# The opening of an mLSTM and window-attention encoder: modulated tiles made in pairs on two engines, products taken as tiles come, the prompt's sums on GpSimd

## The chip, the cores and the metric

The kernel runs on one core of a Trainium2 chip. The metric is the device time of one execution in microseconds (us); lower is better. The engines are TensorE (PE in the profile; its weight loads are PEld), VectorE (DVE), ScalarE (ACT), GpSimd (POOL) and SyncE (SP), which here issues the DMAs.

## What is computed

A two-layer encoder runs over two sequences, a prompt of 256 tokens and a sample of 512, with 1024 channels. Each has a conditioning vector `c`; layer 0 mixes with a chunked mLSTM in both directions, layer 1 with windowed attention, and each layer ends with a convolutional feed-forward block. The part that the change touches is the start of layer 0:

```python
mod = jax.nn.silu(c) @ adaln_w[l] + adaln_b[l]
sh1, sc1, g1, sh2, sc2, g2 = [t[:, None, :] for t in jnp.split(mod, 6, axis=-1)]
h = rmsnorm(x, norm_g[l, 0]) * (1 + sc1) + sh1
...
proj = h @ w_in          # q, k, v, o and the gates of the mLSTM
```

The gates go through a log-sigmoid, a running sum and a running maximum along the tokens before the mLSTM's chunks can be weighted.

## The kernel before

**Layout.** Activations lie with channels on the 128 partitions and tokens along the free axis: eight channel tiles (`KC = 8`) of 768 tokens, the prompt in columns 0 to 255, the sample in 256 to 767. `RANGES` cuts the tokens into three ranges of 256: two of the sample, then the prompt.

**Products.** Each operand is split into a high part (`hh`, `whi`; rounded to the fast float format) and a low part (`hl`, `wlo`; the rest). A product of two tiles is three matmuls: high weight with high activation, high with low, low with high. `fp_copy_split` (L255) makes the parts: a cast on ACT, a subtraction on DVE. In the profile `hh` and `hl` are named `zh` and `zl`.

**Order.** Most instructions are ordered by a planner that simulates a time line at build time and lets whatever is ready there go first, by place in the program; each engine then runs its own queue strictly in that order. Inside a `manual_schedule` block the named engines take the order in which the code is written, and `issue_after` puts an instruction behind another on its engine.

**The opening, in `first` (L1508).** The sample's ranges are loaded and normalized (`Norm`, L89: squares on ACT, sums of tiles on POOL, the sum over partitions by small matmuls with a constant, the root on POOL, a broadcast by matmuls, a multiplication on DVE). Between them `adaln(0, 0)` (L388) multiplies the silu of `c` with sixteen weight rows of 512 KB; its result is copied out by DVE and ACT, transposed, and gives `mod` (shift) and `gain`. Then `modulate` (L561) applies gain and shift to each tile of the sample on DVE in place and splits it.

**The window, in `mlstm` (L633).** Three weight tiles go first: the gates' (`gw`) and the two halves of head 0's queries, through `window` (L310). It goes range by range, in a range weight tile by weight tile, and there over the channels; so each weight tile is finished with a range at a different time. The prompt is normalized beside it (`Norm` with all eight squares summed on TensorE, applied by `modulated`, L540): its steps are traced at points that `tick` chooses between the products. After a sequence's last range the results leave PSUM, by `gates` (L644) or by `keep` (L649). Weights are staged in `raw` tiles (five slots), their parts in `whi` and `wlo` (three slots each); small temporaries of the norms lie in `nt` tiles (eight slots).

**Behind it.** The gates run through Abs, Exp and Ln on ACT (L666 to L668) and six groups of scans and differences on DVE (L669 to L680); then come the two halves of head 0's keys (`gemmT`, L292), with four PSUM banks, and its values (`gemmN`, L331). The modulation of layer 1 (`adaln_v`, L484) fills DVE's gaps: per weight row two operations of 1024 columns, taken a row at a time.

Of the kernel before, what the change touches and what calls it, by code (L numbers as in the profile page):

```python
# [88 lines left out]
class Norm:  # L89
# [13 lines left out]
    def x(self, c):  # L103
        return self.xt[c // 4][:, c % 4, self.rng[0] : self.rng[1]]
# [62 lines left out]
class Net:  # L167
# [219 lines left out]

    def adaln(self, l, th):  # L388
# [16 lines left out]
        ps = self.ps()  # L405
        for i in range(2 * KC):
            k, h = divmod(i, 2)
            cur = fetch(i)
            for g in range(2):
                r0 = 32 * (2 * h + g)  # L410
                self.mm(
                    ps[r0 : r0 + 32, :], self.silc[:, k, :], cur[:, g * 512 : (g + 1) * 512], k == 0, k == KC - 1
                )
# [4 lines left out]
        nc.vector.tensor_copy(sb[0], ps[:, :256])  # L418
        nc.scalar.copy(sb[1], ps[:, 256:])
        pt = self.ps()  # L420
        for b in range(4):
            nc.tensor.transpose(
                pt[:, b * P : (b + 1) * P], sb[b // 2][:, (b % 2) * P : (b % 2 + 1) * P], self.ident
            )
# [5 lines left out]
        if th == 0:  # L430
            for s in range(2):
# [52 lines left out]
    def adaln_v(self, l, pool):  # L484
# [9 lines left out]
        for grp, k in rows:  # L494
# [5 lines left out]
            for s in range(2):  # L500
                w = self.silc[:, k, s : s + 1]
                if k == 0:
                    nc.vector.tensor_scalar(acc[:, s], row, w, None, ALU.mult)
                else:
                    stt(acc[:, s], row, w, acc[:, s], ALU.mult, ALU.add)  # L505
# [127 lines left out]
    def mlstm(self, pool, gw, xt):  # L633
# [211 lines left out]


# [661 lines left out]
    def first(self, pool):  # L1508
# [13 lines left out]
        for rng in RANGES[:2]:  # L1522
            self.modulate(xt, rng, 0, 0)
# [140 lines left out]
```

## The time and the profile before

| | |
|---|---|
| median of three runs | 1846.66 us (1844.48 to 1851.62) |
| profiled execution | 1845.79 us, of which the profiled span is 1843.8 |
| mean granted TensorE clock | 0.992 of full speed |
| TensorE busy | 1794.3 us, 97% |
| VectorE / ScalarE / GpSimd busy | 74% / 49% / 26% |
| DMA | 184.48 MB, 332 GB/s in the first fortieth of the span |

Times in the profile count from the start of the span. A line of the timeline gives start, length, engine, the line of the code, the operation, the tile written and those read, and in brackets how long the engine had idled and what released it. A line such as L253 is a helper's: all products made through `mm` carry it, so they are told apart by their tiles.

### The profile page before, as it was taken

To read this page: it belongs to the slowest core of one execution; us is meant where nothing else is said; L and a number is where in the kernel's file an instruction comes from. 1 tells how busy PE (TensorE), PEld (TensorE's weight loads), DVE (VectorE), ACT (ScalarE), POOL (GpSimd) and SP (SyncE) were. 2 spreads that over 40 slices of the span, in tenths; PEclk is the share of its full clock that TensorE was granted. 3 is DMA by queue.
4 is the path that set the end of the run, shared out by engine and by line. 5 is a ranking of instruction groups with operands and counts; after the bars stand their busy time and mean duration, and the time that the engine had idled before them with its cause. 6 is when DMAs were issued, how large, how long until landed. Compare 5 with 4: busy or idle time off the path is not lost.

```text
span 1843.8 us, 28933 instructions
## 1 busy us (share of the span) xinstructions
PE 1794.3 (97%) x11290; PEld 1657.0 (90%) x11290; DVE 1373.0 (74%) x2101; ACT 898.0 (49%) x1815; POOL 481.6 (26%) x386
## 2 busy tenths in 40 slices
PE   6999999999999999999999999999999999999997
PEld 3987887888998999999999999889989999999997
DVE  4755676886689777777777757766898777787776
ACT  4443443444456444444444556765564444444443
POOL 1001001021024333333331313430134333333322
PEclk8999999999999999999999999999999999999999
DMA  8343556546212221222223321124122222222212
GB/s 332 114 149 133 172 195 226 169 137 211 98 46 77 72 65 64 69 68 68 69 69 93 104 83 50 53 94 136 48 81 69 69 69 69 69 69 69 69 35 69
DMA packets 64245, 184.48 MB, mean 100 GB/s; under 512 B 6167, under 2 KB 23831, under 8 KB 64108
## 3 DMA queue, kind: packets, MB, share of 16 engines
q1 hardware_dynamic: 64108, 182.63, 30.2%
q8 instruction: 89, 1.46, 0.3%
q14 instruction: 48, 0.39, 0.1%
HBM read 176.17 MB, written 6.43 MB: 99 GB/s over the span
## 4 chain that ended last, share of the span: by engine, by line
PE 86%; DVE 6%; DMA 3%; ACT 2%; issue 1%; POOL 1%; SPq 0%; POOLq 0%; ACTq 0%
PE ps L253 27%; PE pa L253 25%; PE ps L1161 10%; PE ps L1164 10%; PE ps L1162 10%; PE pa L1000 1%; DVE wlo L260 1%; DMA raw<-in_w_dram 1%; DMA slab<-in_x_dram 1%; DVE slab L589 1%; DMA slab<-in_adaln_w_dram 1%; DVE ada L505 0%; PE pa L1162 0%; PE pa L1164 0%; PE pa L1161 0%
## 5 line engine op out<-in xcount | busy, mean ns | idle before, releaser
L259 ACT CAST whi<-raw 128x1024 fp32r<-128x1024 f32 x237 | 248.7, 1051 | 347.3 <-PE pa L253 161.4
L260 DVE TENSOR_TENSOR wlo<-raw,whi 128x1024 fp32r<-128x1024 f32 x237 | 320.5, 1353 | 114.7 <-ACT whi L259 112.5
L253 PE MATMUL pa<-slab,whi 128*128 128x256 f32 (+1 forms) x1472 | 346.5, 331 | 3.2 <-DVE slab L589 3.2
L253 PEld LDWEIGHTS pa<-slab,whi 128*128 128x128 f32 x1472 | 252.7, 188 | 27.6 <-DVE slab L589 4.7
L589 DVE SCALAR_TENSOR_TENSOR slab<-pa,mod,slab 128x256 f32<-128x256 f32 (+1 forms) x368 | 211.5, 593 | 70.8 <-PE pa L253 70.5
L253 PE MATMUL pa<-slab,wlo 128*128 128x256 f32 (+1 forms) x736 | 233.8, 330 | 0.0
L253 PE MATMUL ps<-zh,whi 128*128 128x256 f32 (+1 forms) x560 | 188.9, 338 | 1.8 <-ACT whi L259 1.2
L253 PE MATMUL ps<-zh,wlo 128*128 128x256 f32 (+1 forms) x560 | 184.0, 330 | 1.4 <-DVE wlo L260 1.4
L253 PE MATMUL ps<-zl,whi 128*128 128x256 f32 (+1 forms) x560 | 184.9, 332 | 0.0
L1161 PE MATMUL ps<-zh,whi 128*128 128x384 f32 x504 | 172.3, 342 | 3.7 <-ACT nt L1232 1.9
L1162 PE MATMUL ps<-zl,whi 128*128 128x384 f32 x504 | 169.9, 337 | 1.8 <-DVE zl L1118 1.8
L1164 PE MATMUL ps<-zh,wlo 128*128 128x384 f32 x504 | 169.0, 335 | 0.0
L253 PEld LDWEIGHTS pa<-slab,wlo 128*128 128x128 f32 x736 | 138.5, 188 | 13.1 <-DVE wlo L260 0.4
L1197 POOL TENSOR_TENSOR raw<-raw,raw 128x512 f32<-128x512 f32 x40 | 51.9, 1298 | 330.8 <-DVE wlo L260 259.4
L253 PE MATMUL ps<-slab,whi 128*128 128x384 f32 x512 | 132.3, 339 | 2.2 <-ACT sg L841 1.3
L1394 POOL TENSOR_TENSOR slab<-slab 128x772 f32<-128x772 f32 x44 | 86.4, 1967 | 171.7 <-DVE slab L1382 159.8
L1381 DVE SCALAR_TENSOR_TENSOR slab<-slab,cstt,slab 128x771 f32<-128x771 f32 x88 | 105.4, 1199 | 26.7 <-ACT slab L1379 26.6
L505 DVE SCALAR_TENSOR_TENSOR ada<-raw,silc,ada 128x1024 f32<-128x1024 f32 x84 | 112.1, 1372 | 14.5 <-DMA raw<-in_adaln_w_dram 14.4
L253 PEld LDWEIGHTS ps<-zh,whi 128*128 128x128 f32 x560 | 107.2, 192 | 15.1 <-issue 4.4
L253 PEld LDWEIGHTS ps<-zl,whi 128*128 128x128 f32 x560 | 107.3, 192 | 12.0 <-issue 3.4
L253 PEld LDWEIGHTS ps<-zh,wlo 128*128 128x128 f32 x560 | 107.2, 192 | 11.6 <-DVE wlo L260 2.3
L1194 POOL TENSOR_TENSOR raw<-raw 128x512 f32<-128x512 f32 x40 | 63.1, 1578 | 196.5 <-DMA raw<-in_w_dram 168.8
(291 smaller groups left out, 4269.5 us busy)
## 6 DMA issues: line engine op xcount, KB each, us to landing
raw<-in_w_dram SPq DMA_DIRECT2D x208, 512.0 KB, 3.7
raw<-in_adaln_w_dram SPq DMA_DIRECT2D x84, 512.0 KB, 4.5
slab<-in_x_dram SPq DMA_DIRECT2D x12, 512.0 KB, 6.5
slab<-in_adaln_w_dram SPq DMA_DIRECT2D x12, 512.0 KB, 10.3
slab<-mrows SPq DMA_DIRECT2D x8, 384.0 KB, 5.4
xs<-slab SPq DMA_DIRECT2D x6, 512.0 KB, 3.6
bt<-brow SPq DMA_DIRECT2D x16, 192.0 KB, 3.2
slab<-xs SPq DMA_DIRECT2D x6, 512.0 KB, 6.0
```

The lines of the kernel that those rows point to most:

```text
L253: self.nc.tensor.matmul(out, lhsT, rhs, start=start, stop=stop)
L259: nc.scalar.copy(hi, src)
L260: return nc.vector.tensor_tensor(lo, src, hi.bitcast(F32), ALU.subtract)
L505: stt(acc[:, s], row, w, acc[:, s], ALU.mult, ALU.add)
L589: self.nc.vector.scalar_tensor_tensor(x, o, self.mod[l][:, gc + c, q : q + 1], x, ALU.mult, ALU.add)
L1161: mm(o, wh[:, k], hi[k], start=start and k == 0, stop=False, skip_group_check=True)
L1162: mm(o, wh[:, k], lo[k], start=False, stop=False, skip_group_check=True)
L1164: mm(o, wl[:, k], hi[k], start=False, stop=k == 3, skip_group_check=True)
L1194: tt(q[2], q[2], q[3], ALU.add)
L1197: tt(q[0], q[2], q[0], ALU.subtract)
L1381: stt(y[:, 1:], u[:, :-1], w(0), y[:, 1:], ALU.mult, ALU.add)
L1394: nc.gpsimd.tensor_tensor(y, y, yrow[:, j], ALU.mult)
```

## The change

- **adaLN.** The two halves of its result are copied into two separate temporaries instead of two halves of one `raw` tile. After every channel from the fourth on, products of a constant tile with itself (`warm`) follow on TensorE into a bank that is overwritten later: six each, one after the last channel, and five more behind the last transpose. Each sequence's gain is made right behind its own shift.
- **Sample.** `modulate` is gone. In the new function `opening`, ACT modulates the odd channels (in place, by a scale and a bias) and DVE the even ones; ACT casts each tile, DVE makes the low part. All of it stands pair by pair in an order written out for TensorE, ACT and DVE. In the first range the gates' products follow each pair, those of the second weight tile one pair later, and the rest at the end; the parts of the second and third weight tile are made at fixed places in between. In the second range all three tiles' products follow each pair.
- **Prompt.** Its squares stand in the second range, four behind each of the first two pairs, and POOL adds all eight up. The sum over partitions follows the second range's products; then, channel by channel, DVE and ACT make the high part, TensorE takes six products, and low part and three products follow one channel later. All results leave PSUM at the end.
- **Layer 1.** The first rows of `adaln_v` stand behind the prompt's last low part on DVE.

```diff
+    def warm(self, o, n):
+        for _ in range(n):
+            self.mm(o[:, :P], self.ones, self.ones, True, True)
...
+            if h and k > 2:
+                with self.tc.issue_after(last.ins):
+                    self.warm(pt, 6 if k < KC - 1 else 1)
...
-        sb = self.stg.tile([P, 2, 256], F32, tag="raw", name=self.nm("sb"), bufs=5)
-        sb = [sb[:, z] for z in range(2)]
+        sb = [self.tmp([P, 256]) for _ in range(2)]
...
                 if k == 0:
-                    nc.vector.tensor_scalar(acc[:, s], row, w, None, ALU.mult)
+                    with self.tc.issue_after(self.opened.ins):
+                        nc.vector.tensor_scalar(acc[:, s], row, w, None, ALU.mult)
...
-        ws = [(gw, gates)] + [(w, keep(qt0, 0, c)) for c, w in self.halves(U_MIN)]
+        raws = [self.load(U_MIN, h) for h in range(2)]
         self.load_x(io["x"], RANGES[2:], xt)
         nc.sync.dma_start(self.kct[:, P:], io["kc"][:, P : 3 * P])
-        norm = Norm(self, xt, PROMPT, self.modulated(0, 0), KC)
-        for c in range(KC):
-            norm.square(c)
-        self.start(PROMPT, norm.stages())
-        self.window(ws)
+        self.opening(xt, gw, raws, (gates, keep(qt0, 0, 0), keep(qt0, 0, 1)))
...
+    def opening(self, xt, gw, raws, sinks):
...
+        low = lambda i: tt(lo[i], raws[i], hi[i].bitcast(F32), ALU.subtract)
+        high = lambda i: nc.scalar.copy(hi[i], raws[i])
...
+        norm = Norm(self, xt, r2, keep_factor, 0)
+        factor = norm.stages()
+        next(factor)
...
+            def made(c):
+                if c % 2:
+                    act(x(c), x(c), AF.Identity, scale=gain(c, q), bias=shift(c, q))
+                else:
+                    nc.vector.tensor_scalar(x(c), x(c), gain(c, q), shift(c, q), ALU.mult, ALU.add)
+
+            cast = lambda c: nc.scalar.copy(h(c), x(c))
+            lower = lambda c: tt(self.hl[:, c, c0:c1], x(c), h(c).bitcast(F32), ALU.subtract)
...
+        with self.tc.manual_schedule(engines={eng.PE, eng.Activation, eng.DVE}):
+            for i in range(3):
+                bank[i, 0] = self.ps()
+            with self.tc.issue_after(self.turned.ins):
+                self.warm(bank[0, 0], 5)
+            made, cast, lower = sample(r0)
+            made(1)
+            made(0)
+            for c in range(0, KC, 2):
+                cast(c)
+                cast(c + 1)
+                if c + 2 < KC:
+                    made(c + 2)
+                for k in (c, c + 1):
+                    mm(r0, 0, 0, 0, k)
+                    mm(r0, 0, 1, 0, k)
+                if c == 0:
+                    high(0)
+                lower(c)
+                lower(c + 1)
+                if c + 2 < KC:
+                    made(c + 3)
+                for k in (c, c + 1):
+                    mm(r0, 0, 0, 1, k, k == KC - 1)
+                for k in (c - 2, c - 1):
+                    if k >= 0:
+                        mm(r0, 1, 0, 0, k)
+                        mm(r0, 1, 0, 1, k)
+            high(1)
...
+            made, cast, lower = sample(r1)
...
+                if c < 4:
+                    for k in range(2 * c, 2 * c + 4):
+                        norm.square(k)
+            next(factor)
+        next(factor, None)
...
+        with self.tc.manual_schedule(engines={eng.PE, eng.DVE}):
+            for i in range(3):
+                bank[i, 1] = self.pa()
+            late = []
+
+            def later():
+                c, t = late.pop()
+                self.opened = stt(
+                    self.hl[:, c, c0:c1], t, shift(c, q), self.hh[:, c, c0:c1].bitcast(F32), ALU.add, ALU.subtract
+                )
+                for i in range(3):
+                    mm(r2, i, 0, 1, c, c == KC - 1)
+
+            for c in range(KC):
+                t = self.tmp([P, c1 - c0])
+                stt(t, xt[c // 4][:, c % 4, c0:c1], gain(c, q), got[r2], ALU.mult, ALU.mult)
+                act(self.hh[:, c, c0:c1], t, AF.Identity, bias=shift(c, q))
+                for i in range(3):
+                    mm(r2, i, 0, 0, c)
+                    mm(r2, i, 1, 0, c)
+                if late:
+                    later()
+                late.append((c, t))
+            later()
+        for i in range(3):
+            sinks[i](0, bank[i, 0])
+            sinks[i](1, bank[i, 1][:, :256])
...
-        for rng in RANGES[:2]:
-            self.modulate(xt, rng, 0, 0)
```

More of the change, by code (lines that the diff above doesn't have):

```diff
@@ L403, in fetch @@
             return hold[:, z]
-        ps = self.ps()
+        ps, pt = self.ps(), self.ps()
         for i in range(2 * KC):
@@ L410, in adaln @@
                 r0 = 32 * (2 * h + g)
[L411 to L413 removed]
+                last = nc.tensor.matmul(
+                    ps[r0 : r0 + 32, :], self.silc[:, k, :], cur[:, g * 512 : (g + 1) * 512],
+                    start=k == 0, stop=k == KC - 1,
+                )
+            if h and k > 2:
+                with self.tc.issue_after(last.ins):
+                    self.warm(pt, 6 if k < KC - 1 else 1)
             if i < 2 * KC - 1 and h:
                 yield
[L416 to L417 removed]
+        sb = [self.tmp([P, 256]) for _ in range(2)]
         nc.vector.tensor_copy(sb[0], ps[:, :256])
         nc.scalar.copy(sb[1], ps[:, 256:])
[L420 removed]
         for b in range(4):
[L422 removed]
+            self.turned = nc.tensor.transpose(
                 pt[:, b * P : (b + 1) * P], sb[b // 2][:, (b % 2) * P : (b % 2 + 1) * P], self.ident
@@ L429, in adaln @@
             nc.vector.tensor_tensor(dst[:, :, :, s], src[:, :, :, s], ab, ALU.add)
-        if th == 0:
-            for s in range(2):
+            if th == 0:
                 nc.vector.scalar_tensor_tensor(
```

56 lines of the change are left out of this document (added).

## The prediction

> **What bounds the kernel now.** First the page: TensorE is busy 97% of the span, so a gain has to come out of the few stretches where it idles or runs on a low clock.
>
> ```profile
> span 1843.8 us, 28933 instructions
> PE 1794.3 (97%) x11290; PEld 1657.0 (90%) x11290; DVE 1373.0 (74%) x2101; ACT 898.0 (49%) x1815; POOL 481.6 (26%) x386
> ```
>
> Then the windows of the opening, cut at the places where TensorE's pace changes (columns: length, busy time and instructions of PE, PEld, DVE, ACT, POOL, granted clock, DMA share, GB/s).
>
> ```profile
> 19.50:22.50 3.00, 0.06 (x4) 0.05 (x4) 2.39 (x1) 2.54 (x8) 1.58 (x3) 1.00 1.06 424
> 22.50:26.00 3.50, 3.50 (x10) 0.70 (x11) 0.00 (x0) 0.05 (x1) 2.05 (x3) 0.54 1.03 412
> 36.40:42.60 6.20, 5.65 (x25) 5.36 (x25) 6.20 (x20) 5.90 (x18) 0.00 (x0) 0.50 0.77 307
> 42.60:46.40 3.80, 3.80 (x19) 3.80 (x19) 3.80 (x10) 1.99 (x5) 0.58 (x1) 0.50 0.23 57
> 46.40:70.70 24.30, 24.30 (x204) 24.30 (x203) 18.71 (x32) 11.36 (x19) 2.70 (x1) 0.99 0.30 97
> 70.70:87.50 16.80, 16.80 (x98) 14.75 (x97) 13.73 (x19) 8.21 (x12) 0.00 (x0) 1.00 0.34 105
> ```
>
> The 216 products of the opening (three weight tiles, three ranges, eight channels, three products each) run from 42.6 to 70.7. At full clock one takes 24.30 / 204 = 0.119 us, at half clock 3.80 / 19 = 0.200. Nothing ahead of the modulation can be shortened much: DMA is at full share while the adaLN rows come in. The timeline shows why the products don't start when the first activation is there:
>
> ```profile
> 32.71 1.05 PE L253 MATMUL ps<-slab,silc 128*32 128x512 f32 x4 [0.25 <-DMA slab<-in_adaln_w_dram]
> 33.81 0.42 DVE L418 COPY sb<-ps 128x256 f32<-128x256 f32 x1 [1.30 <-PE ps L253]
> 34.27 0.37 ACT L419 COPY sb<-ps 128x256 f32<-128x256 f32 x1 [5.67 <-DVE sb L418]
> 36.49 0.58 PE L253 MATMUL ps<-zh,whi 128*128 128x256 f32 x1 [0.18 <-ACT zh L259]
> 37.53 5.28 PE L253 MATMUL pa<-inv,nt 128*128 128x2 f32 x24 [0.46 <-ACT nt L110]
> 35.59 5.26 DVE L565 TENSOR_SCALAR slab<-slab,gain,mod 128x256 f32<-128x256 f32 x16
> 40.75 2.44 DVE L260 TENSOR_TENSOR zl<-slab,zh 128x256 fp32r<-128x256 f32 x7
> ```
>
> One product runs at 36.49; then the prompt's sums hold TensorE for 5.28 us, and DVE makes all sixteen modulated tiles before the first low part at 40.75. The opening has 36.5 to 70.7 for 216 x 0.119 = 25.7 us of work: 8.5 us are the most it can give back on TensorE, and 0.5% of the kernel, about what a measurement of it can tell from no change, is 9.2 us.
>
> Last the chain of waits behind the opening. TensorE is dense to 87.5 and idles only until 88.03, but that wait ends a long chain of gates:
>
> ```profile
> 66.07 0.47 ACT L646 ACTIVATE slab<-pa,cstt 36x256 f32<-36x256 f32 x1
> 73.85 0.95 DVE L670 TENSOR_TENSOR slab<-slab 36x768 f32<-36x768 f32 x1 [2.68 <-ACT slab L668]
> 85.93 0.85 ACT L780 ACTIVATE slab<-slab 36x768 f32<-36x768 f32 x1 [4.20 <-DVE slab L779]
> 86.69 1.58 ACT L259 CAST slab<-ps 128x512 fp32r<-128x512 f32 x4
> 88.03 0.39 PE L253 MATMUL ps<-whi,zh 128*128 128x256 f32 x1 [0.45 <-DVE slab L260]
> ```
>
> The prompt's gates leave PSUM at 66.07, their logarithm and scans fill ACT and DVE to 85.9, and ACT empties the four banks of the key tiles only behind that exp (86.69); the value products wait for a bank. From gates to values it is 88.03 - 66.07 = 22.0 us. So TensorE and this chain arrive within half a microsecond of each other: shortening one alone buys little.
>
> **The change part by part.** *Start.* The two halves of the modulation row now lie in two tiles, so ACT's copy (34.27, released by DVE's) can run beside DVE's: 0.4 us; the sample's gain is made before the prompt's shift, one tiny DVE operation less: 0.1. First product at 36.0 instead of 36.49.
>
> *Constant products.* Six after each of four channels of adaLN, two passes each. Their nearest row is four passes in 0.71 us:
>
> ```profile
> 28.41 0.71 PE L253 MATMUL pa<-kct,nr 128*128 128x128 f32 x4
> 27.29 1.06 PE L253 MATMUL ps<-slab,silc 128*32 128x512 f32 x8
> ```
>
> Six cost at most 2.1 us. The last set stands before rows 14 and 15; two waiting rows run together in 1.06 (27.29), and row 15 lands near 32.7 anyway, so I take nothing. At half clock they could hold the last row back by 1 us; that end goes into the range.
>
> *First range.* ACT's order is written out: modulate channel 1, cast 0, cast 1, then the high part of weight tile 1, then everything else. That cast needs its raw tile. Its load, and what ACT's casts take:
>
> ```profile
> 29.58 0.36 SPq L268 DMA_DIRECT2D raw<-in_w_dram  x1
> raw<-in_w_dram SPq DMA_DIRECT2D x1, 512.0 KB, 9.0
> 39.83 1.04 ACT L259 CAST whi<-raw 128x1024 fp32r<-128x1024 f32 x1
> 38.60 1.32 ACT L259 CAST zh<-slab 128x256 fp32r<-128x256 f32 x4
> ```
>
> Issued at 29.58, landed 9.0 later: 38.6. I expect the same issue order after: five raw slots are taken by four adaLN rows and the gate weights, while every other load has its slot at once, so the weights go last as now. ACT has its first two casts done by 36.2, then stands 2.4 us for a DMA that before nobody waited for; queued behind it are all further casts. Cast to 39.65, one modulation and one cast of 0.33 each and the handover: channel 2 reaches TensorE at 40.4. TensorE had six products (0.7 us) and idles from 37.1: **+3.3 us**. Such a gap lowers the clock: after 2.94 us of idling at 19.5 it was 0.54. The recovery at 42.60 cost 19 x (0.200 - 0.119) = 1.5: **+1.5**. The Trainium skill (TensorE: Matmul & The Clock Gate, "What's actually happening") has the clock fall only after an idle window of about 3.4 us; by that this gap might go free and the sum would be 1.5 us less; the trace's shorter gap speaks against it. After 40.4 a pair of channels costs ACT three times 0.33 and DVE about as much, while TensorE has ten products, 1.2 us: TensorE sets the pace. Two sample ranges end at 36.0 + 3.3 + 1.5 + 144 x 0.119 = 57.9.
>
> *Prompt's factor.* The squares go to ACT in the second range and the sums to POOL (seven adds), out of TensorE's 5.28 us. But two last sums, the root, the broadcast and the first modulation now follow the second range's last product, in TensorE's own order:
>
> ```profile
> 12.60 1.50 PE L253 MATMUL pa<-inv,nt 128*128 128x2 f32 x12
> 14.38 0.72 POOL L152 TENSOR_TENSOR nr<-nr,mhalf 128x2 f32<-128x2 f32 x1 [3.66 <-DVE nr L151]
> 15.96 2.74 DVE L558 TENSOR_TENSOR slab<-slab,pa 128x256 f32<-128x256 f32 x8 [1.66 <-DMA slab<-in_adaln_w_dram]
> 51.62 3.32 ACT L550 ACTIVATE zh<-nt,mod 128x256 fp32r<-128x256 f32 x8 [7.04 <-DVE nt L548]
> 45.82 3.29 POOL L152 TENSOR_TENSOR nr<-nr,mhalf 128x2 f32<-128x2 f32 x1 [17.47 <-DVE nr L151]
> ```
>
> Four passes are 0.5; from the end of the sums (14.1) to the first use of the broadcast (15.96) 1.86; one DVE and one ACT operation 1.0. **+3.4 us**, where before all of it lay beside products. The weight slots are full, so no other product can fill it. With DVE busy the root took 3.29 instead of 0.72; here DVE is idle, since the layer-1 rows are held back, so I take 0.72. Then 72 x 0.119 = 8.6: the opening ends at 57.9 + 3.4 + 8.6 = **69.9**, against 70.7.
>
> *Tail.* Before, the range's tiles ended one after another, and the next weights were cast in the slot of the first:
>
> ```profile
> 65.11 1.05 ACT L259 CAST whi<-raw 128x1024 fp32r<-128x1024 f32 x1 [2.21 <-PE pa L253]
> 67.06 0.85 ACT L666 ACTIVATE slab<-slab 36x768 f32<-36x768 f32 x1
> ```
>
> Now all three end with channel 7, and all three slots come free at 69.9. TensorE waits for a cast: 1.1 us if ACT takes it first, 2.1 behind the two gate rows (0.47 each), 3.7 behind the other evacuations and the Abs too. I take 2.1: key products from 72.0, and with 16.7 of them plus the 0.6 wait, values at 89.3: +1.3. The gates too now leave at 69.9 instead of 66.07; their 22.0 us give 91.9, or 92.9 with the key cast inside the chain: +3.9 to +4.9. The diff moves neither the scans nor the key banks' evacuation, so I lean to the chain and take **+3.5**.
>
> *Layer 1's rows.* Three of them ran on DVE beside the opening; now they wait for the prompt's last low part:
>
> ```profile
> 54.24 1.41 DVE L503 TENSOR_SCALAR ada<-raw,silc 128x1024 f32<-128x1024 f32 x2
> 65.63 2.48 DVE L505 SCALAR_TENSOR_TENSOR ada<-raw,silc,ada 128x1024 f32<-128x1024 f32 x2 [2.00 <-DMA raw<-in_adaln_w_dram]
> 88.00:106.00 18.00, 17.97 (x151) 17.80 (x151) 3.36 (x8) 2.52 (x7) 3.68 (x2) 1.00 0.25 75
> 126.00:136.00 10.00, 10.00 (x57) 8.85 (x57) 10.00 (x13) 2.99 (x8) 0.00 (x0) 0.87 0.75 252
> ```
>
> That is 1.41 + 2 x 2.48 = 6.4 us. While ACT does the logarithm, and in 88 to 106 with 14.6 us idle, DVE has room; I take nothing, with 6.4 as the other end. Held back, the rows keep raw slots longer, and SP's queue stands at the next row's load with the gate rows' round trip through DRAM behind it:
>
> ```profile
> 84.94 0.37 SPq L682 DMA_DIRECT2D mrows<-slab  x1
> 91.20 3.68 POOL L700 TENSOR_TENSOR slab<-slab,kct 128x768 f32<-128x768 f32 x2 [42.10 <-PE ps L253]
> 106.57 0.41 ACT L760 ACTIVATE E<-slab,aT 128x128 f32<-128x128 f32 x1 [0.59 <-DVE aT L690]
> ```
>
> Its masks were done at 94.9 and first read at 106.6: 11.7 us of cover, more than two rows' wait. Nothing for it.
>
> The sum is made on the profiled execution: 1845.79 (its span and 2.0 around it) + 3.5 = 1849.3. The median of the runs lies 0.87 above it: 1850.
>
> **The rivals.** *Faster: the raw tiles are there in time* (chance 0.2). If the weights are issued ahead of the prompt's input, ACT never stands; 3.3 and 1.5 fall away and the opening ends at 65.1. Values come at 84.5 by TensorE (-3.5) and 87.1 by the chain (-0.9): about 1843 to 1846. For it: the diff writes these loads first and takes one tile off the raw slots. Against: they stood first in the code before as well and left last.
>
> *No change* (0.2). ACT casts the key weights first and empties the key banks ahead of the exp; then values come at 69.9 + 1.1 + 16.7 + 0.6 = 88.3, +0.3: 1847. Against: the queue order that 86.69 shows.
>
> *Slower: layer 1's rows fall into 116 to 136* (0.15). In 126 to 136 DVE has no idle time (10.00 of 10.00); if the planner places the three rows there, attention's small DVE operations wait 6.4 us behind them: 3.5 + 6.4, 1856.6. It decides once DVE finds no 6.4 us between 70 and 106; the 14.6 idle speak against it.
>
> **How the numbers follow.** The forecast has 0.45; its own range is 1847 to 1853 (+1.3 to +4.9, with 1.5 either way for the clock). The whole range takes in the rivals: 1842 to 1857. Faster by over 0.5% (under 1837.4) is beyond even a perfect opening: 0.03. Slower by over 0.5% (over 1855.9) is most of the third rival and a stacked tail: 0.14. Within: 0.83.
>
> **What would show it.** ACT idle some 2.4 us before the first weight cast, released by the weight DMA, and TensorE idle 3 us near 37 to 40 on a half clock after; a second gap of 3.4 near 58 with the root inside; a third of about 2 released by a weight cast near 70; the value products near 91. I am wrong if the raw tile lands before 36.5, if the products run dense from 36 to 62, or if the values start before 86.

## The result, and the profile after

The changed kernel takes 1853.92 us (median of six runs, 1849.88 to 1857.48) against 1846.51 for the kernel before (six runs beside it, 1844.48 to 1851.62): a ratio of 1.0037, 95% interval 1.0023 to 1.0051. It is slower by 7.4 us, inside "within 0.5%". The profiled execution is the lowest of the six, 1849.88, with a span of 1847.7:

```profile
span 1847.7 us, 29002 instructions
PE 1794.6 (97%) x11322; PEld 1658.4 (90%) x11322; DVE 1372.6 (74%) x2093; ACT 899.7 (49%) x1823; POOL 488.8 (26%) x393
```

TensorE is as busy as before (1794.6 against 1794.3), so of the 3.9 us between the two spans 3.6 are idle time; what a low clock costs is part of the busy time. The windows of the opening and of the products behind it, with the cuts that the prediction used:

```profile
36.40:42.60 6.20, 5.03 (x36) 4.41 (x36) 4.12 (x15) 5.26 (x14) 0.00 (x0) 1.00 0.82 322
42.60:46.40 3.80, 3.80 (x34) 3.80 (x33) 3.65 (x7) 2.14 (x5) 0.00 (x0) 1.00 0.21 52
46.40:70.70 24.30, 20.91 (x172) 20.42 (x170) 15.99 (x32) 13.56 (x33) 6.42 (x8) 1.00 0.16 50
70.70:87.50 16.80, 15.55 (x73) 13.09 (x74) 16.23 (x18) 10.76 (x12) 0.00 (x0) 0.90 0.51 170
```

The half clock of the opening is gone (1.00 where it was 0.50) and 36.40 to 46.40 holds 70 matmuls instead of 44 (ten of the 70 are constant products, 24 of the 44 were the prompt's sums). What was won there is given back in 46.40 to 70.70, where TensorE now idles 3.4 us, and from 70.70 on, where it idles and runs on 0.90. The start, in the timeline of SP, TensorE and ACT (the third line is the first of the two loads, with its time from issue to landing):

```profile
24.45 1.58 SPq L268 DMA_DIRECT2D raw<-in_w_dram  x2
26.94 1.66 SPq L379 DMA_DIRECT2D slab<-in_x_dram  x2
raw<-in_w_dram SPq DMA_DIRECT2D x1, 512.0 KB, 11.2
32.80 1.60 PE L253 MATMUL ps<-ones 128*128 128x128 f32 x12
34.33 1.09 PE L415 MATMUL ps<-slab,silc 128*32 128x512 f32 x8
36.06 0.37 ACT L426 COPY nt<-ps 128x256 f32<-128x256 f32 x1 [6.79 <-DVE nt L425]
38.32 0.39 PE L253 MATMUL ps<-zh,whi 128*128 128x256 f32 x1 [0.28 <-ACT zh L893]
38.48 1.04 ACT L858 CAST whi<-raw 128x1024 fp32r<-128x1024 f32 x1
40.37 0.39 PE L253 MATMUL ps<-zh,whi 128*128 128x256 f32 x1 [0.87 <-ACT zh L893]
```

Twelve constant products stand ahead of adaLN's last row, which ends at 35.4 (before: 33.76); the first product is at 38.32 (36.49). Part of that is older than the change: adaLN's first product ran at 10.23 in this execution and at 9.61 in the one profiled before, and over the fourteen profiled executions of all kernels of this case it lies between 9.07 and 10.23. ACT's copy of the modulation row (36.06) still waits for DVE's, which ends at 35.96. ACT's weight cast (L858) follows its neighbour with nothing in brackets: no wait for the transfer, and TensorE waits 0.87 us for the next channel. The transfer was early because its place in SP's queue has changed. Before, the prompt's input went out ahead of it (with the load itself at 29.58):

```profile
23.71 1.66 SPq L379 DMA_DIRECT2D slab<-in_x_dram  x2
```

Now the first weight load goes out at 24.45, ahead of the prompt's input, and lands 11.2 us later, at 35.6. The gap ahead of the prompt's factor:

```profile
57.22 0.50 PE L253 MATMUL pa<-inv,nt 128*128 128x2 f32 x4
58.00 0.71 POOL L152 TENSOR_TENSOR nr<-nr,mhalf 128x2 f32<-128x2 f32 x1 [3.95 <-DVE nr L151]
58.76 0.71 PE L253 MATMUL pa<-kct,nr 128*128 128x128 f32 x4 [1.04 <-POOL nr L152]
60.89 0.39 PE L253 MATMUL pa<-zh,whi 128*128 128x256 f32 x1 [1.42 <-ACT zh L979]
```

From the last sample product (57.2) to the first prompt product (60.89) it is 3.7 us. Last the tail, ACT, DVE and TensorE in order of time:

```profile
69.57 0.47 ACT L652 ACTIVATE slab<-pa,cstt 36x256 f32<-36x256 f32 x1 [3.01 <-PE pa L253]
70.83 1.04 ACT L259 CAST whi<-raw 128x1024 fp32r<-128x1024 f32 x1
71.92 0.50 PE L253 MATMUL ps<-zh,whi 128*128 128x512 f32 x1 [2.15 <-ACT whi L259]
72.04 1.99 ACT L259 CAST whi<-raw 128x1024 fp32r<-128x1024 f32 x2
73.92 0.84 ACT L668 ACTIVATE slab<-slab 36x768 f32<-36x768 f32 x1
78.24 0.94 ACT L670 ACTIVATE slab<-slab,ones 36x768 f32<-36x768 f32 x1
78.03 2.47 DVE L511 SCALAR_TENSOR_TENSOR ada<-raw,silc,ada 128x1024 f32<-128x1024 f32 x2
80.42 0.94 DVE L672 TENSOR_TENSOR slab<-slab 36x768 f32<-36x768 f32 x1
92.11 0.84 ACT L782 ACTIVATE slab<-slab 36x768 f32<-36x768 f32 x1 [6.81 <-DVE slab L727]
92.86 1.58 ACT L259 CAST slab<-ps 128x512 fp32r<-128x512 f32 x4
93.48 2.93 PE L253 MATMUL pa<-slab,slab 128*128 128x512 f32 x6 [2.31 <-ACT slab L259]
96.20 0.36 PE L253 MATMUL ps<-whi,zh 128*128 128x256 f32 x1
```

Read it as a ladder against before: gates leave PSUM at 69.57 (66.07, +3.5); Abs at 73.92 (67.06, +6.9), because three weight casts stand ahead of it; the difference on DVE at 80.42 (73.85, +6.6), now behind a layer-1 row; the exponential behind the scans, called exp F from here on, at 92.11 (85.93, +6.2). Behind exp F ACT empties the key banks, and for these TensorE waits 2.31 us. The order behind the keys has changed too: six products of queries and keys (93.48) and six small transposes of the gates (from 90.61 on), which before ran from 105.5 on, now stand ahead of the value products, and these start at 96.20 (88.03). TensorE's clock after the two waits, in windows:

```profile
72.00:74.00 2.00, 1.97 (x6) 1.49 (x7) 2.00 (x2) 2.00 (x4) 0.00 (x0) 0.62 0.00 0
74.00:76.00 2.00, 2.00 (x7) 1.61 (x7) 2.00 (x4) 1.98 (x3) 0.00 (x0) 0.53 0.83 248
92.00:96.00 4.00, 2.52 (x6) 2.04 (x7) 2.36 (x8) 2.33 (x5) 0.00 (x0) 0.62 0.48 121
```

So TensorE's account is: 1.2 later into the keys (71.92 against 70.70); 2.4 longer in them (71.92 to 91.17, 19.25 us, against 70.70 to 87.58, 16.88), of which the two rows of low clock explain 2 x 0.38 + 2 x 0.47 = 1.7 and the transposes, work brought forward, 0.5; 1.9 more waiting behind them (2.31 against 0.45); and about 1.3 for 2.5 us of work near half clock up to 96. That is 6.8, or 6.3 without the transposes. The sigmoid near the end of layer 0 starts 6.8 us later than before (375.2 against 368.4). The spans differ by 3.9 only, since before's profiled execution was the slower of the two from there on (1475.4 us from the sigmoid to the end against 1472.5); the difference of the medians is 7.4.

### The profile page after: what moved, and what is told of

It is laid out like the page before. It is cut to its first block, busy times and chain, and to the rows that moved or that the text cites. A ratio compares the mean times of both kernels' runs of the same rounds, so it can differ in the third digit from the quotient of the medians.

```text
span 1847.7 us, 29002 instructions
## 1 busy us (share of the span) xinstructions
PE 1794.6 (97%) x11322; PEld 1658.4 (90%) x11322; DVE 1372.6 (74%) x2093; ACT 899.7 (49%) x1823; POOL 488.8 (26%) x393
## 4 chain that ended last, share of the span: by engine, by line
PE 83%; DVE 7%; issue 4%; ACT 2%; DMA 2%; POOL 1%; SPq 0%; POOLq 0%; DVEq 0%; ACTq 0%
PE pa L253 24%; PE ps L253 24%; PE ps L1305 10%; PE ps L1308 10%; PE ps L1306 10%; PE pa L1144 1%; DMA raw<-in_w_dram 1%; DVE ada L511 1%; DVE wlo L260 1%; PE ps L415 1%; DVE slab L595 1%; DMA raw<-in_adaln_w_dram 1%; PE pa L1308 0%; PE pa L1305 0%; PE pa L1306 0%
## 5 line engine op out<-in xcount | busy, mean ns | idle before, releaser
L253 PE MATMUL ps<-zh,wlo 128*128 128x256 f32 (+1 forms) x560 | 179.3, 328 | 1.9 <-DVE wlo L260 1.9
L253 PE MATMUL ps<-zl,whi 128*128 128x256 f32 (+1 forms) x560 | 180.4, 331 | 0.0
```

Source lines behind the costliest of these rows:

```text
L253: self.nc.tensor.matmul(out, lhsT, rhs, start=start, stop=stop)
```

## The experiments

Four theories were named as the runs went on. **A**: the three tiles that end together lengthen the tail (gates late, weight casts ahead of Abs, key banks behind exp F), and TensorE waits for it. **B**: the layer-1 rows that now stand in the tail on DVE. **C** (later **E**, by one place): transfers behind the opening, above all a layer-1 row that DVE waits for. **D**: the gap ahead of the prompt's factor and the low clock that may follow it. Medians are of five or more runs of the kernel, those of before 1846.3 to 1846.8. Each ratio is known to 0.0009 to 0.0014, so two changed kernels whose times differ by less than about 3 us can't be told apart.

### The third tile last

```diff
-                for i in range(3):
+                for i in range(2):
                     mm(r2, i, 0, 1, c, c == KC - 1)
...
-                for i in range(3):
+                for i in range(2):
                     mm(r2, i, 0, 0, c)
                     mm(r2, i, 1, 0, c)
...
+            for c in range(KC):
+                mm(r2, 2, 0, 0, c)
+                mm(r2, 2, 0, 1, c)
+                mm(r2, 2, 1, 0, c, c == KC - 1)
```

> The changed kernel, but in the prompt's range only the first two weight tiles take their products channel by channel; the third follows after them, so the tiles no longer end together. Theory A (the time is lost behind the opening, because all three tiles end with the last channel: gates leave PSUM late, the key weights find no free slot): the gates leave PSUM about 2 us earlier than in the changed kernel (67.5 instead of 69.6), the first key weight is cast while the third tile still runs, TensorE's idle stretch of 2.2 us before the key products and the low clock after it go, and the kernel is 2 to 4 us faster than the changed one, a ratio of 1.0015 to 1.0025 to the kernel before. Theory B (the time is lost because layer 1's held-back rows stand ahead of the gates' scans on VectorE): the scans start no earlier than in the changed kernel, 80.4 us, and the ratio stays at 1.003 to 1.004.

Measured: 1855.84, ratio 1.0053 (1.0041 to 1.0065). Against the changed kernel's 1853.92 that is inside the noise. The wait for the key cast is gone, but nothing is won:

```profile
60.00:62.00 2.00, 1.66 (x8) 1.67 (x9) 2.00 (x6) 1.14 (x3) 0.00 (x0) 0.50 0.00 0
68.99 0.47 ACT L652 ACTIVATE slab<-pa,cstt 36x256 f32<-36x256 f32 x1 [2.99 <-PE pa L253]
```

In this profile the clock stood at 0.50 from 60 to 66, behind the same gap that cost the changed kernel's profiled execution nothing, so the gates leave at 68.99 and exp F is at 91.53 (92.11). The early gates were never there. Neither theory's number; the run says only that A can't be tested while the gap and its clock stand ahead of it.

### Layer 1's rows not held back

```diff
-                    with self.tc.issue_after(self.opened.ins):
-                        nc.vector.tensor_scalar(acc[:, s], row, w, None, ALU.mult)
+                    nc.vector.tensor_scalar(acc[:, s], row, w, None, ALU.mult)
```

> The changed kernel with layer 1's first row no longer held behind the prompt's last low part. Theory B: the rows run in the opening again, none stands between the logarithm and the scans, the scans start at about 78 instead of 80.4 and the kernel is 2 to 6 us faster than the changed one (ratio 1.000 to 1.0025). Theory A: the scans start at most 1 us earlier, the ratio stays at 1.003 to 1.004; if the rows fall between the sums of the prompt and the root, the gap before the prompt's products grows by up to 2.5 us.

Measured: 1857.60, ratio 1.0062 (1.0049 to 1.0076), 3.7 us slower than the changed kernel. The rows now fall between DVE's low parts, for which TensorE waits (1.38 us is the longest), and the gates leave at 73.60:

```profile
53.57 0.62 PE L253 MATMUL ps<-zl,whi 128*128 128x256 f32 x3 [1.38 <-DVE zl L893]
73.60 0.47 ACT L651 ACTIVATE slab<-pa,cstt 36x256 f32<-36x256 f32 x1 [3.00 <-PE pa L253]
```

No row is left in the tail, and yet it is later: B as the whole cause falls. Held back, the rows cost less than where the planner puts them by itself.

### The prompt's sums early

```diff
+                if c == KC - 2:
+                    next(factor)
...
+                if c == KC - 2:
+                    next(factor, None)
...
-            next(factor)
-        next(factor, None)
```

> The changed kernel with the prompt's last sums ahead of the products of the second range's last channel pair, and the broadcast of the root behind the first twelve of them, so that the root runs beside products. The gap of 3.7 us before the prompt's products (57.2 to 60.9) shrinks to under 1 us and the opening ends at about 66.6 instead of 69.8. If what follows hangs on the opening's end (theory A, and B as well), all of the 3 us reach the end: ratio about 1.002 to the kernel before. If a chain that does not start there sets the pace behind (a third theory, C: the transfers and the planned order further on), less than 1 us reaches the end: 1.003 to 1.004.

Measured: 1853.86, ratio 1.0041 (1.0028 to 1.0054), no change to the changed kernel. The sums and the broadcast run beside the sample's products now, but TensorE still idles 2.26 us (before this edit 1.04 and 1.42):

```profile
58.06 0.60 ACT L262 ACTIVATE slab<-ps 128x512 fp32r<-128x512 f32 x1
58.55 0.50 ACT L981 ACTIVATE zh<-nt,mod 128x256 fp32r<-128x256 f32 x1
59.10 0.39 PE L253 MATMUL pa<-zh,whi 128*128 128x256 f32 x1 [2.26 <-ACT zh L981]
```

What ended last was not the factor: ACT first evacuates the sample's tiles (three operations from 56.65 on) and modulates the prompt's first channel only behind them. The 1.2 us that TensorE no longer spends on sums and broadcast in the gap are lost again to the clock, which fell behind it (0.85 and 0.50 in 58 to 62; the changed kernel's profile has 1.00). Two causes lay side by side, and taking one away showed the other.

### No constant products

```diff
-            if h and k > 2:
-                with self.tc.issue_after(last.ins):
-                    self.warm(pt, 6 if k < KC - 1 else 1)
```

> The changed kernel without the constant products between the adaLN rows (the five behind the last transpose stay). If they hold the last row back, its products end at about 33.8 instead of 35.4 and the first product of the opening starts at about 36.5 instead of 38.3; the weight cast on ScalarE then waits for its DMA until 38.6, so that at most 0.5 us of it reaches the end of the opening. If the clock falls to half in the gap before 40, the first range takes 1.5 us longer and the kernel is 1 to 2 us slower than the changed one (ratio 1.0045); if it stays at full speed the ratio is 1.003 to 1.004.

Measured: 1853.99, ratio 1.0038 (1.0026 to 1.0050). The first product is at 36.73 against 38.32, and the first prompt product at 59.33 instead of 60.89; but here the clock fell behind the gap (0.50 in 60 to 62), the gates leave at 69.28 against 69.57, and the time is the same. Of the 1.6 us at the start half is not the constant products' doing: in this execution adaLN's first product already ran 0.84 us earlier (9.39 against 10.23), ahead of any of them. Counted from there, adaLN's last row ends after 24.4 us here and after 25.2 in the changed kernel, so they hold it back by some 0.8; in the run with the sums early, which has them, the first product is at 36.92.

The other two questions of this run have an answer too. The clock is 1.00 from 36.4 to 46.4 here as well, so it is not the constant products between the rows that took the half clock away; whether the five behind the last transpose did, or the prompt's sums that are gone from there, is open. And ACT's weight cast does not wait until 38.6:

```profile
36.90 1.05 ACT L855 CAST whi<-raw 128x1024 fp32r<-128x1024 f32 x1
```

Its load went out at 23.85 and landed 10.2 us later, at 34.1.

### The shared end alone, in the kernel before

```diff
+            if q:
...
+                    for k in range(KC):
...
+                        for i, (wh, wl) in enumerate(parts):
```

> The kernel before, with one edit: in the prompt's range of the opening the products of the three weight tiles are taken channel by channel instead of tile by tile, so that the three tiles end together; the opening's start, the layer-1 rows and every transfer stay as before. Theory A (the tail behind a shared end is the price of the change): TensorE has done its 216 products at about 70.7 as before, but the gates leave PSUM at 70 to 71 instead of 66.07, the Abs stands behind the weight casts on ScalarE (72 or later instead of 67.06), exp F comes at 90 to 92 instead of 85.93, and the kernel is 4 to 6 us slower than before: 1850.5 to 1852.5. Theory C (the later start of the transfers behind the opening is what counts): 1846 to 1848, since no transfer is moved. Theory D (the gap ahead of the prompt's factor and the low clock behind it are the price, the tail rides along): 1846.5 to 1848.5, the gates' chain later but no gap in the products.

Measured: 1857.38, ratio 1.0064 (1.0050 to 1.0078), 11.1 us slower than before: one edit, which takes the prompt's range channel by channel over all three tiles, costs more than the whole change.

```profile
70.53 0.47 ACT L663 ACTIVATE slab<-pa,cstt 36x256 f32<-36x256 f32 x1
73.93 0.84 ACT L683 ACTIVATE slab<-slab 36x768 f32<-36x768 f32 x1
90.90 0.84 ACT L797 ACTIVATE slab<-slab 36x768 f32<-36x768 f32 x1 [8.79 <-DVE slab L742]
```

Gates, Abs and exp F stand where A had them (70 to 71, 72 or later, 90 to 92), with the opening, its rows and its transfers as before: C and D fall as main causes. The size was beyond A's 4 to 6: the sigmoid near the end of layer 0 is 5.8 us late, inside A's range, and some 5 us more are lost after it (1480.4 us to the end; the thirteen other profiles have 1472.4 to 1476.2), in part in 1000 to 1100 (a granted clock of 0.95, where before had 0.98 and the changed kernel 1.00). Why is open.

### The gap closed

The early sums, and ACT's evacuation of the sample's tiles behind the prompt's last modulated tile.

```diff
-                act(self.hh[:, c, c0:c1], t, AF.Identity, bias=shift(c, q))
+                made_last = act(self.hh[:, c, c0:c1], t, AF.Identity, bias=shift(c, q))
...
+        with self.tc.issue_after(made_last.ins):
+            for i in range(3):
+                sinks[i](0, bank[i, 0])
         for i in range(3):
-            sinks[i](0, bank[i, 0])
             sinks[i](1, bank[i, 1][:, :256])
```

> The changed kernel with the prompt's sums taken ahead of the sample's last pair of channels, the broadcast behind that pair's first twelve products, and ScalarE's evacuation of the sample's tiles put behind the prompt's last modulated tile. Theory A (shared end): the gap of 3.7 us ahead of the first prompt product goes to under 0.5, the opening ends at 66 instead of 69.6, and everything behind it is 3 to 4 us earlier: exp F at 87.5 to 88.5, the kernel 1849.5 to 1851; that is still 3 to 4.5 above the kernel before, because the three tiles still end together. Theory C: 1853 to 1855, for the transfers' order behind the opening isn't changed. Theory D (gap and clock): back to the kernel before, 1846 to 1848.5.

Measured: 1852.43, ratio 1.0033 (1.0020 to 1.0045).

```profile
58.78 0.39 PE L253 MATMUL pa<-zh,whi 128*128 128x256 f32 x1 [0.47 <-ACT zh L981]
67.47 0.47 ACT L652 ACTIVATE slab<-pa,cstt 36x256 f32<-36x256 f32 x1 [0.97 <-PE pa L253]
92.44 2.37 PE L253 MATMUL pa<-slab,slab 128*128 128x512 f32 x6 [4.01 <-ACT slab L259]
```

The gap is gone (0.47) and the gates leave 2.1 us earlier, but exp F comes at 91.07, 1.0 earlier, and TensorE, earlier at the end of the keys, waits 4.01 instead of 2.31. D falls: the time does not go back to before. By the medians the gap is worth 1.5 us, which is inside the noise. The rest is held up by the tail on ACT and DVE.

### Abs, Exp and Ln ahead of the casts

The list marks which of the next three weight casts wait for Ln: not the first key cast, but the second and the values'.

```diff
+        if self.behind and self.behind.pop(0):
+            with self.tc.issue_after(self.ln.ins):
+                self.fp_copy_split(hi, lo, src)
...
+        self.ln = nc.scalar.activation(ex, ex, AF.Ln, bias=self.ones[0:G, 0:1])
+        self.behind = [False, True, True]
```

> The changed kernel with one edit: on ScalarE the gates' Abs, Exp and Ln stand ahead of the second key cast and the value casts instead of behind them. Theory A (the gates' chain sets the end): Ln ends at 77 to 78 instead of 79.2, exp F comes 1 to 2 us before 92.1, and the kernel is 1 to 2 us faster than the changed one: 1852 to 1853. If the casts are what counts (TensorE waits for the second key tile and then for the value weights): a new wait of 2 to 4 us between the two key tiles near 80, and 1854 to 1857. Theory C: no difference to the changed kernel, 1853.5 to 1854.5.

Measured: 1854.86, ratio 1.0045 (1.0033 to 1.0058), no gain.

```profile
75.97 0.94 ACT L675 ACTIVATE slab<-slab,ones 36x768 f32<-36x768 f32 x1
82.55 1.20 DVE L681 TENSOR_TENSOR_SCAN slab<-slab,slab 4x512 f32<-4x512 f32 x1
93.36 0.84 ACT L788 ACTIVATE slab<-slab 36x768 f32<-36x768 f32 x1 [9.21 <-DVE slab L733]
```

Ln ends 2.3 us earlier (76.9 against 79.2), but the casts that ACT now does behind it send their low parts (twice 1.22) and a layer-1 row (2.47) to DVE ahead of the first scan: 82.55 against 81.40, and exp F is 1.25 late. The chain has two queues, and clearing one filled the other.

### All three together

The early sums with the late evacuations, the third tile last, and Abs, Exp and Ln ahead of the casts: the diffs above, in one kernel.

> The changed kernel with three edits together: the gap ahead of the prompt's factor closed as in the kernel with the sums taken early and the evacuations late; the third weight tile's prompt products behind those of the other two, so that the gates leave early and the next weights are cast beside products; and Abs, Exp and Ln ahead of the second key cast. Theory A: gates leave at 62 to 64, the products end at 66 without a wait for the key cast, exp F at 83 to 85, the kernel 1842.5 to 1845.5, below the kernel before (about 1846.5). Theory C: 1852 to 1855. Theory D (gap and clock alone): 1846 to 1848.5, as in the kernel with the gap closed alone.

Measured: 1854.54, ratio 1.0043 (1.0030 to 1.0055). Gates leave at 65.93 and Ln is at 72.70, where before had it, yet exp F comes at 90.09: DVE has a row and two low parts between its difference (73.67) and the first scan (79.28). TensorE, early, waits 5.18 us for the key banks at 91.45 and then runs at 0.50 from 92 to 96. A's number is missed; by the trace DVE's queue and the banks are what was left of the tail, and the next two runs take one each.

### The key banks ahead of exp F

The changed kernel with one edit: the sum ahead of exp F waits for the key tiles' last low part, so that ACT and DVE empty the banks first.

```diff
-                nc.vector.tensor_tensor(F, F, M, ALU.add)
+                with self.tc.issue_after(keys_kept.ins):
+                    nc.vector.tensor_tensor(F, F, M, ALU.add)
```

> The changed kernel with one edit: the sum ahead of exp F, and with it exp F, stand behind the emptying of the four key banks instead of ahead of it; the gates' chain itself is as late as in the changed kernel. Theory A (TensorE waits for the key banks behind the gates' chain, 2.31 us at 93.48, and runs on a low clock after): the first products of queries and keys come at 91.5 to 92.5, the wait is about 1 us, the clock after it higher, and the kernel 1.5 to 3 us faster than the changed one: 1851 to 1852.5. Theory E (DVE waits for a row of layer 1 that lands near 125.6 in the changed kernel, and what was won ahead of that is waited away): the products come earlier, but the reciprocals near 133.9 do not, and the time stays at 1853 to 1854.5.

Measured: 1849.14 (twelve runs), ratio 1.0011 (1.0001 to 1.0021): 4.8 us of the 7.4 are back. In windows:

```profile
88.00:92.00 4.00, 4.00 (x32) 3.67 (x30) 3.91 (x5) 0.72 (x2) 0.00 (x0) 1.00 0.47 135
92.00:96.00 4.00, 4.00 (x31) 3.68 (x30) 3.19 (x8) 0.24 (x1) 0.00 (x0) 1.00 0.20 68
```

TensorE has no wait from 74 to 120, and from 80 on its clock stays at 1.00 (0.72 in 74 to 80, behind the wait for the key cast, which is still there). The gates' chain is as late as ever and exp F, now at 99.76, later. So the chain's lateness by itself costs little; what costs is that key banks stand behind it. Some 2.3 us against before are left. The gain is beyond A's 1.5 to 3, which had counted the wait and part of the low clock only. The layer-1 row lands at 123.37 instead of 125.59: it follows TensorE and doesn't lead it, and E falls here.

### The rows behind all scans

The kernel with all three edits, and layer 1's first three rows behind the last scan.

```diff
-            scan(M[32:36, b][:, ::-1], a[32:36, b][:, ::-1], z[32:36, b], 0.0, ALU.max, ALU.add)
+            self.opened = scan(M[32:36, b][:, ::-1], a[32:36, b][:, ::-1], z[32:36, b], 0.0, ALU.max, ALU.add)
```

> The kernel with the gap closed, the third tile last and Abs, Exp, Ln ahead of the second key cast (1854.54), with one edit more: layer 1's first three rows on DVE stand behind all scans, so that between Ln and exp F DVE has the scans and two low parts of weights alone, as in the kernel before. Theory A: exp F comes at 85.5 to 87 (90.09 without this edit, 85.93 before), TensorE waits under 1.5 us ahead of the values, and the kernel is at 1845 to 1848, level with the kernel before. Theory E: exp F as early, but the rows now fall behind 86 on DVE and a row that DVE or TensorE waits for lands at 125 or later; 1851 to 1855 all the same.

Measured: 1849.93 (twelve runs), ratio 1.0016 (1.0007 to 1.0026): 4.6 us faster than without this edit. The scans end at 86.4 instead of 89.1. But exp F is at 89.81, not at A's 85.5 to 87, since a row and a low part slipped ahead of its sum, and the banks' low parts stand behind another row:

```profile
92.86 0.58 PE L254 MATMUL ps<-whi,zh 128*128 128x256 f32 x1 [4.19 <-DVE slab L261]
```

So the size of the gain is not explained by exp F, nor by E, whose row lands at 125.48 as it did without the edit (125.60). The visible difference is DVE's order behind that row: GpSimd's first root of the heads' norm is at 148.5 here and at 151.3 there. The rows' place matters; through which of the two it pays was not settled.

### All that helped, and a control

The last two runs: all edits together, with the rows behind the key banks' low parts; and the kernel before with exp F behind the banks (the diff shown above for that, in the kernel before).

```diff
-            keys_kept = self.kept
+            keys_kept = self.opened = self.kept
```

> All that helped put together: the changed kernel with the gap ahead of the prompt's factor closed, the third tile's prompt products last, Abs, Exp and Ln ahead of the second key cast, exp F behind the emptying of the key banks, and layer 1's first rows on DVE behind the key banks' low parts. Theory A (the tail is the price, the opening itself is shorter than before): key products end near 86.5, the next products follow with under 0.7 us of waiting, about a microsecond earlier than the 88.03 of the kernel before, and the time is 1843 to 1846.5, at or just below the kernel before (about 1846.8). Theory E (what is won is waited away where DVE waits for layer 1's row): the row lands at 123 or later against 121.26 before, and the time is 1848 to 1851, as with the key banks first alone.

> The kernel before with one edit: exp F behind the emptying of the four key banks. It tells whether that edit is worth something by itself or only heals what the change has done. Theory A: in the kernel before TensorE waits only 0.45 us for the key banks, so at most 0.5 us is to be had: 1845.8 to 1847.3. If the order of exp F and banks were worth as much there as in the changed kernel (4.8 us): 1841 to 1843.

Measured: 1847.18 (eleven runs), ratio 1.0001 (0.9992 to 1.0010), for all edits; 1846.18, ratio 0.9997 (0.9988 to 1.0006), for the control. Neither can be told from before. Of the two theories for all edits E misses, for the row lands at 119.73, ahead of the 121.26 of before; A has the early products, but not its wait of under 0.7 us nor, by 0.7 us, its time.

```profile
86.82 0.39 PE L254 MATMUL ps<-whi,zh 128*128 128x256 f32 x1 [1.69 <-DVE slab L261]
119.73 2.48 DVE L516 SCALAR_TENSOR_TENSOR ada<-raw,silc,ada 128x1024 f32<-128x1024 f32 x2 [2.63 <-DMA raw<-in_adaln_w_dram]
```

With the tail mended the change is level with before: the opening ends 3 us earlier (key products from 67.61 against 70.70), and the value products start at 86.82 instead of 88.03, 1.2 us earlier, behind a wait of 1.69 for low parts on DVE. None of the 1.2 is left at the sigmoid (368.6 against 368.4; the control has it at 370.2, so single profiles differ there by 2 us without a difference in the time). The control shows that the order of banks and exp F is worth nothing where the chain is on time (0.4 of 1846.6, inside the interval), so the 4.8 us it saved in the changed kernel were damage done by the change.

## Why the prediction was right or wrong

1850.0 was forecast, in a range of 1842 to 1857 and for the forecast alone 1847 to 1853; it was 1853.92, inside the first and 0.9 outside the second. The direction and the tail's mechanism held, the tail is nearly twice as large as its term, and the first range went as the faster rival had it. By its steps:

- **Start, 36.0: wrong, 38.32.** The 0.5 us of the split copies and the shorter chain never came: ACT's copy waits for DVE's as before, though they write two tiles (36.06, 0.1 behind the end of DVE's), and from the end of adaLN's last row to the first product it is 2.90 us against 2.73. Both copies read the same bank; whether that is the reason no run tells. The constant products, taken as nothing with a bound of 1 us, cost some 0.8 and so kept to the bound. The other 0.6 is the later start of adaLN in this execution.
- **First range, +3.3 and +1.5: wrong.** The step that failed is "the same issue order after". The weight load left SP ahead of the prompt's input, landed at 35.6 and not at 38.6, and ACT's cast found its tile there. The late start has no part in it: without the constant products the cast comes at 36.90 and doesn't wait either. What was left is the 0.87 us of the cast itself, and the clock stayed at 1.00. The faster rival's condition was met, and its argument (the diff writes these loads first and takes one tile off the raw slots) was the right one; which of the two did it was not tested.
- The two errors cancel by luck: the sample's ranges end at 57.2, forecast 57.9.
- **Factor, +3.4: right in size (3.7), with a hidden partner.** The root took 0.71 with DVE idle, as forecast. But ACT's evacuations make nearly the same gap without it, as the run with early sums showed (2.26 us of idling).
- **Gates at 69.9, keys at 72.0: right** (69.57, 71.92), the wait by its own working (2.15), the place by the two errors that cancel.
- **Tail, +3.5: right in kind, mis-sized, and this is the miss.** The forecast leaned to the chain with +3.9 to +4.9 at the values. Measured is +6.2 at exp F, since all three casts, the value weights' too, stood ahead of Abs (1.99 us more than the one cast counted). TensorE's own side, +1.3, is +3.6 up to the end of the keys, 0.5 of it work brought forward. And the clock was charged once, at 40, where it did not fall, and not behind the two waits of the tail, where it did: 1.7 and 1.3 us.
- **Layer-1 rows, nothing: wrong.** One of them (78.03) stands on DVE ahead of the scans. With ACT's chain mended it is one of three operations that keep the scans back by 4.7 us. Without holding the rows it is worse still.
- **Mask's round trip, nothing:** right for TensorE, which has no wait for it and, with the key banks ahead of exp F, is dense through it. But the 11.7 us of cover are gone: in the changed kernel ACT waits 2.65 us for the rows at 97.09 and 1.31 for a mask at 99.02.
- **Rivals.** The faster one's price (opening at 65.1, 1843 to 1846) was never paid out: with the gap closed the opening ends at 67.5 and the time is 1852.43. The tail stood behind it, and the rival, with the values at 87.1 by the chain, had the forecast's small tail too. "No change" asked for the key banks ahead of the exp; that edit, by itself, gives 1849.14. So the sentence against it, that the queue order of 86.69 would stay, was the sentence that decided. The row rival (136, DVE full) did not occur as told.
- **Signs.** The ones for the second gap, for the third and for the late values were seen (the values at 96.20 instead of 91, as other products now stand ahead of them); those for the raw tile (ACT idle, half clock near 40) were not. One sign of being wrong came true, the raw tile landing before 36.5 (35.6), and one by half: the products are dense but for 0.87 from 38.3 up to 57.

## What to carry to other kernels

When tiles that ended one after another are made to end together, count what was hidden under the stagger: the next weights' casts, the first evacuations and the chain that the first tile feeds now all queue at one moment, on engines that take them in order. Ask of each queue what stands ahead of the critical operation and whether it has to: here one edit (empty the banks first) gave back 4.8 of 7.4 us while the chain itself stayed late. And don't judge one of several serial waits by taking it away alone: closing the gap, or moving the chain on ACT, brought nothing beyond the noise until DVE's queue and the banks were mended too. Last, a term that hangs on one load needs that load's place in the issuing queue after the change: here the load went out 5 us earlier, and 3.9 of the 4.8 us of the first range's term fell away.

## What the runs showed of the hardware

The granted clock can fall behind idle times shorter than the prediction had to go by (2.94 us): 2.15 us ahead of 71.92 was followed by 0.62 and 0.53, and 2.26 us in the run with early sums by 0.85 and 0.50:

```profile
58.00:60.00 2.00, 0.90 (x5) 0.90 (x6) 1.31 (x3) 1.91 (x5) 0.00 (x0) 0.85 0.00 0
60.00:62.00 2.00, 2.00 (x11) 2.00 (x11) 2.00 (x6) 0.93 (x2) 0.00 (x0) 0.50 0.00 0
```

The same gap doesn't always do it. The wait of 2.15 or 2.16 us ahead of the key products stands in seven of the profiles; in five the clock fell behind it, and in two, with the rows not held back and with the gap closed, it stayed at 1.00. And 1.04 and 1.42 us of idling with 0.71 of products between them left the clock at 1.00 in the changed kernel's profile, and took it to 0.50 from 60 to 66 in the run with the third tile last. The Trainium skill (TensorE: Matmul & The Clock Gate, "What's actually happening") lets the clock fall after an idle window of about 3.4 us, counted by a window that runs free. The measured 2.15 us are less than that, and the measurement decides; that the same gap goes either way agrees with a window that runs free, which no run here shows directly. Where it fell behind the wait ahead of the key products it cost 1.5 to 1.7 us (in the changed kernel 2 x 0.38 + 2 x 0.47), so a sum does well to carry such a wait with 0 to 2 us on top.
